# The last tile's second to fourth quarter stores, split by partitions

## The chip, the cores and the metric

The kernel runs on one core of one Trainium2 chip. The metric is the device time of one execution, in microseconds. The time before is 134.82 us, the median of 8 runs that lie between 134.19 and 135.21 us.

A core has five engines that take instructions: TensorE (PE in the profile), VectorE (DVE), ScalarE (ACT), GpSimd (POOL) and SyncE (SP). Transfers between the on-chip memory and DRAM are issued from SP, ACT and POOL, and are carried out by 16 DMA engines that all three share. In the profile, q1 is SP's DMA queue, q10 ACT's, and q0 POOL's; q8 and q14 carry fetches of instructions.

## The reference

Two arrays of 1024 matrices of 64 x 64 are multiplied matrix by matrix:

```python
"a": np.random.randn(1024, 64, 64).astype(np.float32)
"b": np.random.randn(1024, 64, 64).astype(np.float32)
np.matmul(a, b).astype(np.float32)
```

The inputs are 16.8 MB each and so is the output.

## The kernel before

The batch is cut into 16 tiles of 64 matrices. The matrix `b` is loaded a tile at a time (`load_b`, line 96, 1 MB, in turn on SP's and ACT's queue), and `a` two tiles at a time (`load_a`, lines 73 and 77; three quarters of it by POOL with a cast to bf16, one quarter by SP). `regroup` casts and reorders `a`; `transpose` turns it on TensorE and ScalarE copies the result out of PSUM (line 123); `spread` (line 133) writes it on VectorE into a block-diagonal tile; `cast` (lines 144, 149 and 151) makes the bf16 copy of `b`. `multiply` then runs 64 matrix multiplications for a tile into PSUM (line 189), and `evacuate` (line 177) copies the results to the tile's output buffer `o_sb` in on-chip memory, with ScalarE or VectorE.

The order of the work on each engine is the order in which the code is written (`tc.manual_schedule()`). Stores lag one tile behind: after tile t is multiplied, tile t-1 is stored, and tile 15 is stored at the very end.

A tile's output buffer has 128 partitions of 8 blocks (`gh`), each of 1 KB per partition. Tiles 0 to 13 are stored whole, 1 MB each, by POOL. Tile 14 is stored as two halves of 512 KB by SP. The last tile, 15, is multiplied in four quarters of two blocks each, copied out in turn by ScalarE and VectorE, and it is stored as four quarters of 256 KB:

```python
def store_queue(t, lo):
    if t < n_t - 2:
        return nc.gpsimd
    return nc.scalar if t == n_t - 1 and lo % 4 == 0 else nc.sync
```

So quarters 0 and 2 (`lo` of 0 and 4, copied out by ScalarE) are issued by ACT, and quarters 1 and 3 (`lo` of 2 and 6, copied out by VectorE) by SP. The order in which SP takes them is: tile 14's first half, its second half, quarter 1, quarter 3. ACT takes quarter 0 and then quarter 2. All stores are issued on line 166.

The completion of a transfer is counted on a semaphore. Those issued from SP and ACT share eight of these (named DMAHW0 to DMAHW7 in the built program), which are handed out in turn in the order of the program; a transfer that is given one that was used before waits, on its issuing engine, until the earlier transfer of that semaphore has landed. At the end of the program (line 282), SP waits for all of them in a fixed order, and then all engines meet in a closing barrier.

Of the kernel before, what the change touches and what calls it, by code (L numbers as in the profile page):

```python
# [13 lines left out]
def kernel(  # L14
# [27 lines left out]
    o_v = out.rearrange("(t gh x) (mo w) n -> t (x mo) gh (w n)", gh=8, x=8, w=4)  # L42
# [21 lines left out]
# [4 lines that stand above are left out]
# [90 lines left out]
    def multiply(t):  # L158
        at_bd = bd_tiles[t % N_BD][:].rearrange("p j g wl h mo -> p j g (wl h mo)")
        at_bd = at_bd.bitcast(bf16).rearrange("p j g (c u) -> p j g c u", u=2)  # L160
        b_bf = bbf_tiles.pop(t)
        last = t == n_t - 1
        o_sb = o_pool.tile([128, 8, 2, 2, 64], fp32, name="o_sb")

        def put(lo, n):
            store_queue(t, lo).dma_start(  # L166
                out=o_v[t, :, lo : lo + n, :],
                in_=o_sb[:, lo : lo + n].rearrange("p gh j wl n -> p (gh j wl n)"),
            )

        def evacuate(o_ps, gh, n, copies):

            for par in range(2):
                for wl in range(2):
                    src = o_ps[64 * wl : 64 * wl + 64, :, par, :, :]
                    dst = o_sb[64 * par : 64 * par + 64, gh : gh + n, :, wl, :]
                    copies[2 * par + wl](dst, src)  # L177

        for half in range(2):
            if not last:  # L180
                o_ps = o_psum.tile([128, 4, 2, 2, 64], fp32, name="o_ps")
            for g8 in range(8):
                if last and g8 % 4 == 0:
                    o_ps = t_psum.tile([128, 2, 2, 2, 64], fp32, name="at_ps")
                g = 8 * half + g8
                gl = (g8 % 4 if last else g8) // 2
                for j in range(2):
                    for u in range(2):
                        nc.tensor.matmul(  # L189
                            o_ps[:, gl, g % 2, j, :],  # L190
                            at_bd[:, j, g, :, u],
                            b_bf[:, g, 64 * u : 64 * u + 64],
                            start=(u == 0),
                            stop=(u == 1),
                        )
                if last and g8 % 4 == 3:
                    copy = nc.scalar.copy if g8 == 3 else nc.vector.tensor_copy
                    evacuate(o_ps, g // 4 * 2, 2, [copy] * 4)
            if not last:
                copies = [nc.scalar.copy] * 4  # L200
                if half and t % 2:
                    copies[2:] = [nc.vector.tensor_copy] * 2
                evacuate(o_ps, 4 * half, 4, copies)
        if last:
            held[t] = [lambda q=q: put(2 * q, 2) for q in range(4)]
        else:
            whole = t < n_t - 2
            held[t] = [lambda q=q: put(q, 8 if whole else 4) for q in ([0] if whole else [0, 4])]

    with tc.manual_schedule():  # L210
# [18 lines left out]
        for t in range(n_t):  # L229
            s, half = t // 2, t % 2  # L230
            if t + 1 < n_t:
                spread(t + 1)
                cast(t + 1)
            if t + B_AHEAD < n_t:
                load_b(t + B_AHEAD)
            if half == 0 and 0 < s < n_s - 1 - A_AHEAD:
                load_a(s + 1 + A_AHEAD)
            if half == 0 and 0 < s < n_s - 1:
                transpose(s + 1, 1)
            multiply(t)  # L240
            if t == 0:
                regroup(1)
                load_a(A_AHEAD)
                load_a(A_AHEAD + 1)
                transpose(1, 0)
                transpose(1, 1)
            elif t == 1:
                regroup(2)
            elif half == 0 and s + 2 < n_s:
                regroup(s + 2)  # L250
            if half == 1 and s + 2 < n_s:
                transpose(s + 2, 0)
            if t >= HOLD - 1:
                store(t - HOLD + 1)
# [32 lines left out]
```

## Time and profile before

| | |
|---|---|
| time of the profiled execution | 134.82 us |
| its span, first to last instruction | 133.0 us |
| median of 8 runs | 134.82 us (134.19 to 135.21) |
| busy share of the span: PE, DVE, ACT, POOL | 48%, 70%, 66%, 25% |
| mean of DMA traffic over the span | 338 GB/s |
| last tile's last copy | 125.29 to 125.65 us |
| last tile's stores, issue to landing (median) | 7.4 us from SP, 5.6 us from ACT |

How to read it: "busy" counts the time in which an engine works on instructions, while instructions that only issue a transfer or wait are not counted. The DMA row of the page cuts the span into 40 slices and gives the mean busy share of the 16 DMA engines in tenths, 9 standing for 90% or more. The waits name which engine stood still, at which line, and what it was waiting for. The order of time lists instructions by their start, with the time they took; `SPq` and `ACTq` are the issues of transfers on those engines. An answer on DMA for a stretch gives the same kind of 40 digits for that stretch, the rate of each slice, and how many packets were smaller than a given size. Behind these views lie the records of single packets (queue, start, duration, size) and of each step by which a transfer's semaphore went up as its parts landed. The records do not say which of the 16 DMA engines carried a packet.

### The profile page before, as it was taken

To read this page: it belongs to the slowest core of one execution; us is meant where nothing else is said; L and a number is where in the kernel's file an instruction comes from. 1 tells how busy PE (TensorE), PEld (TensorE's weight loads), DVE (VectorE), ACT (ScalarE), POOL (GpSimd) and SP (SyncE) were. 2 spreads that over 40 slices of the span, in tenths; PEclk is the share of its full clock that TensorE was granted. 3 is DMA by queue.
4 is the path that set the end of the run, shared out by engine and by line. 5 is a ranking of instruction groups with operands and counts; after the bars stand their busy time and mean duration, and the time that the engine had idled before them with its cause. 6 is when DMAs were issued, how large, how long until landed. Compare 5 with 4: busy or idle time off the path is not lost.

```text
span 133.0 us, 2837 instructions
## 1 busy us (share of the span) xinstructions
PE 63.2 (48%) x1152; PEld 59.9 (45%) x1152; DVE 93.6 (70%) x120; ACT 87.9 (66%) x161; POOL 32.7 (25%) x43
## 2 busy tenths in 40 slices
PE   0008205960079375279436961866098355761000
PEld 0008105950079374179336961855097354761000
DVE  5621599008999809896899799969999995989000
ACT  3333314999126999959495979696969969089700
POOL 8981000320082070452123003202120402220000
PEclk9999965797557999856985599599959955599555
DMA  3999999999999999999999999999999999999990
GB/s 71 390 329 309 307 296 288 277 305 326 328 326 396 307 318 353 392 384 386 316 278 381 405 390 341 307 321 389 395 393 387 398 392 390 402 405 398 384 343 31
DMA packets 19021, 45.01 MB, mean 338 GB/s; under 512 B 1088, under 2 KB 3136, under 8 KB 19008
## 3 DMA queue, kind: packets, MB, share of 16 engines
q0 software_dynamic: 6832, 20.19, 50.3%
q1 hardware_dynamic: 7120, 14.68, 30.1%
q10 hardware_dynamic: 5056, 9.96, 20.2%
q8 instruction: 9, 0.15, 0.4%
q14 instruction: 4, 0.03, 0.1%
HBM read 33.55 MB, written 16.78 MB: 378 GB/s over the span
## 4 chain that ended last, share of the span: by engine, by line
DMA 54%; DVE 15%; ACT 13%; PE 6%; issue 5%; SPq 1%; ACTq 0%; DVEq 0%
DMA b_sb<-in_b_dram 54%; ACT o_sb L177 9%; DVE at_bd L133 7%; PE o_ps L189 4%; DVE b_bf L144 4%; DVE o_sb L177 3%; PE at_ps L120 2%; ACT at_sb L123 2%; ACT b_bf L144 1%; SPq L90 1%; DVE a_bf L108 1%; ACT b_bf L151 1%; DVE a_bf L111 0%; SPq L96 0%; DVEq L144 0%
## 5 line engine op out<-in xcount | busy, mean ns | idle before, releaser
L177 ACT COPY o_sb<-o_ps 64x512 f32<-64x512 f32 x106 | 61.5, 580 | 10.6 <-PE o_ps L189 9.3
L189 PEld LDWEIGHTS <-at_bd 128*128 128x128 bf16 x1024 | 41.8, 112 | 41.5 <-DVE b_bf L144 26.5
L189 PE MATMUL o_ps<-b_bf,at_bd 128*128 128x64 bf16 x960 | 42.2, 215 | 37.2 <-DVE b_bf L144 24.6
L133 DVE COPY at_bd<-at_sb 32x1024 f32<-32x1024 f32 x64 | 47.4, 741 | 13.5 <-ACT at_sb L123 11.4
L166 POOL DMA_DIRECT2D out_dram<-o_sb x14 | 15.7, 1124 | 58.5 <-ACT at_sb L123 22.7
L120 PE MATMUL at_ps<-identity,a_bf 128*128 128x128 f32 x128 | 20.5, 328 | 18.8 <-DVE a_bf L105 10.6
L120 PEld LDWEIGHTS at_ps<-identity,a_bf 128*128 128x128 f32 x128 | 18.5, 174 | 18.9 <-issue 18.9
L123 ACT COPY at_sb<-at_ps 128x512 f32<-128x512 f32 x32 | 17.5, 589 | 11.3 <-PE at_ps L120 8.5
L144 DVE CAST b_bf<-b_sb 128x2048 bf16<-128x2048 f32 x14 | 17.4, 1245 | 9.6 <-DMA b_sb<-in_b_dram 9.4
L73 POOL DMA_DIRECT2D a_sb<-in_a_dram x21 | 12.9, 628 | 25.3 <-DVE a_bf L108 19.0
L177 DVE COPY o_sb<-o_ps 64x512 f32<-64x512 f32 x14 | 9.6, 689 | 0.3
L108 DVE COPY a_bf<-a_sb 128x3072 bf16<-128x3072 bf16 x7 | 6.7, 953 | 0.0
L144 ACT CAST b_bf<-b_sb 128x2048 bf16<-128x2048 f32 x1 | 1.9, 1898 | 4.7 <-DMA b_sb<-in_b_dram 4.7
L105 ACT CAST a_bf<-o_sb 128x1024 bf16<-128x1024 f32 x2 | 2.1, 1044 | 4.2 <-DMA o_sb<-in_a_dram 4.2
L111 DVE CAST a_bf<-a_raw 128x1024 bf16<-128x1024 f32 x7 | 4.8, 686 | 0.0
L105 DVE CAST a_bf<-o_sb 128x1024 bf16<-128x1024 f32 x2 | 1.5, 772 | 3.7 <-DMA o_sb<-in_a_dram 3.7
L217 DVE MEMSET at_bd<- 128x4096 f32 x1 | 3.5, 3472 | 0.8 <-issue 0.8
L177 DVE COPY o_sb<-at_ps 64x256 f32<-64x256 f32 x8 | 3.4, 422 | 0.5 <-PE at_ps L189 0.4
L151 ACT CAST b_bf<-b_sb 128x512 bf16<-128x512 f32 x2 | 1.1, 616 | 3.4 <-DMA b_sb<-in_b_dram 3.4
L177 ACT COPY o_sb<-at_ps 64x256 f32<-64x256 f32 x8 | 2.9, 366 | 0.1
L214 ACT ACT_TABLE_LOAD x1 | 1.3, 1283 | 2.1 <-issue 2.1
L189 PE MATMUL at_ps<-b_bf,at_bd 128*128 128x64 bf16 x64 | 2.0, 194 | 1.1 <-DVE at_bd L133 1.1
(12 smaller groups left out, 6.1 us busy)
## 6 DMA issues: line engine op xcount, KB each, us to landing
out_dram<-o_sb POOLq DMA_DIRECT2D x14, 1024.0 KB, 21.4
a_sb<-in_a_dram POOLq DMA_DIRECT2D x21, 256.0 KB, 15.8
a_raw<-in_a_dram SPq DMA_DIRECT2D x7, 512.0 KB, 18.5
o_sb<-in_a_dram SPq DMA_DIRECT2D x2, 512.0 KB, 6.9
o_sb<-in_a_dram ACTq DMA_DIRECT2D x2, 512.0 KB, 5.8
out_dram<-o_sb SPq DMA_DIRECT2D x2, 512.0 KB, 7.3
out_dram<-o_sb SPq DMA_DIRECT2D x2, 256.0 KB, 7.4
out_dram<-o_sb ACTq DMA_DIRECT2D x2, 256.0 KB, 5.6
```

Of the source, the lines that this page charges most:

```text
L73: nc.gpsimd.dma_start(out=a_sb[:, h, :, :].rearrange("p v k -> p (v k)"), in_=a_v[s, h])
L105: copy(a_bf[:, :, h, :], a_sb[h].rearrange("p (v k) -> p v k", v=16))
L108: nc.vector.tensor_copy(a_bf[:, :, 0:3, :], cast_sb[:].rearrange("p h v k -> p v h k"))
L111: nc.vector.tensor_copy(a_bf[:, :, 3, :], raw[:])
L120: nc.tensor.transpose(at_ps[:, vo, :], a_cols[:, 4 * vo + 2 * j + wl, :], identity[:])
L123: nc.scalar.copy(at_tiles[s][:, j, :, wl, :, :], at_ps[:].rearrange("p vo (g mp) -> p g mp vo", mp=4),)
L133: nc.vector.tensor_copy(bd[rows, :, :, :, h, :].rearrange("p j g wl mo -> p j (g wl) mo"), at_tiles[t // 2][rows, :, half, :, :, :].rearrange(
L144: (nc.vector.tensor_copy if t else nc.scalar.copy)(b_bf[:], b_sb[:])
L166: store_queue(t, lo).dma_start(out=o_v[t, :, lo : lo + n, :], in_=o_sb[:, lo : lo + n].rearrange("p gh j wl n -> p (gh j wl n)"),)
L177: copies[2 * par + wl](dst, src)
L189: nc.tensor.matmul(o_ps[:, gl, g % 2, j, :], at_bd[:, j, g, :, u], b_bf[:, g, 64 * u : 64 * u + 64], start=(u == 0), stop=(u == 1),)
L217: nc.vector.memset(bd_tiles[0][:], 0.0)
```

## The change

Inside `multiply`, the helper `put`, which issues a store, gets a table of cuts by partition. For the last tile, quarter 1 is stored as partitions 0 to 119 and 120 to 127; quarter 2 as partitions 0 to 125 and 126 to 127; quarter 3 as partitions 0 to 119, 120 to 126, and 127. Quarter 0 and all other tiles are stored as before. The pieces of one quarter are issued one after the other from the same engine, so SP issues five transfers for the last tile in place of two, and ACT three in place of two. The bytes that are written are the same.

```diff
         def put(lo, n):
-            store_queue(t, lo).dma_start(
-                out=o_v[t, :, lo : lo + n, :],
-                in_=o_sb[:, lo : lo + n].rearrange("p gh j wl n -> p (gh j wl n)"),
-            )
+
+            cuts = {2: [0, 120, 128], 4: [0, 126, 128], 6: [0, 120, 127, 128]}.get(
+                lo if last else 0, [0, 128]
+            )
+            for p0, p1 in zip(cuts[:-1], cuts[1:]):
+                store_queue(t, lo).dma_start(
+                    out=o_v[t, p0:p1, lo : lo + n, :],
+                    in_=o_sb[p0:p1, lo : lo + n].rearrange(
+                        "p gh j wl n -> p (gh j wl n)"
+                    ),
+                )
```

In the built program the last stores then stand in this order, with the semaphore that each is counted on and the one that it waits for, beside the copies:

```
SP   tile 14, first half     counted on DMAHW3
SP   tile 14, second half    counted on DMAHW4
SP   quarter 1, 120          counted on DMAHW5
ACT  quarter 0, 128          counted on DMAHW6
SP   quarter 1, 8            counted on DMAHW7, waits for its earlier transfer (a load of b)
ACT  quarter 2, 126          counted on DMAHW0, waits for its earlier transfer (a load of b)
SP   quarter 3, 120          counted on DMAHW1, waits for its earlier transfer (a load of b)
ACT  quarter 2, 2            counted on DMAHW2
SP   quarter 3, 7            counted on DMAHW3, waits for tile 14, first half
SP   quarter 3, 1            counted on DMAHW4, waits for tile 14, second half
```

SP's closing waits stand in the order DMAHW0 to DMAHW7, in both programs. Before, quarter 3 was counted on DMAHW0, quarter 2 on DMAHW7.

## The prediction

> **What bounds the kernel now.** I read the page first, for the totals, then only the tail, because every edited instruction is issued after 123 us of a span of 133.0 us. No instruction ahead of that is moved; the built order of the changed kernel differs from that of before in the last stores of SP and ACT alone. The page's sections 1, 2 and 6 of the kernel before:
>
> ```profile
> span 133.0 us, 2837 instructions
> DMA  3999999999999999999999999999999999999990
> out_dram<-o_sb SPq DMA_DIRECT2D x2, 256.0 KB, 7.4
> out_dram<-o_sb ACTq DMA_DIRECT2D x2, 256.0 KB, 5.6
> ```
>
> The transfers are busy to the last slice but one, and the four quarter stores (256 KB each) take 5.6 to 7.4 us to land. The next view is the order of time from 118 us on:
>
> ```profile
> 120.25 5.44 SPq L166 DMA_DIRECT2D out_dram<-o_sb  x4
> ...
> 124.16 0.40 ACTq L166 DMA_DIRECT2D out_dram<-o_sb  x1
> 124.53 1.12 ACT L177 COPY o_sb<-at_ps 64x256 f32<-64x256 f32 x3
> 125.68 0.38 ACTq L166 DMA_DIRECT2D out_dram<-o_sb  x1
> ```
>
> The last copy and the last issue are over by 126.1. The waits from 117 us on say what follows:
>
> ```profile
> SPq L282 <- DMA out_dram<-o_sb: 5.9, 1, 5.9
> ```
>
> SP, which ends the kernel, stands 5.9 us for stores. The DMA view of 128:130 and then of 130:131 and 131:132 shows how they end:
>
> ```profile
> DMA  9999999999988988977788967687765677644555
> ...
> DMA  2442612111121010101101011010110101011010
> DMA packets 50, 0.04 MB, mean 44 GB/s; under 512 B 7, under 2 KB 50, under 8 KB 50
> ...
> DMA packets 10, 0.01 MB, mean 8 GB/s; under 512 B 2, under 2 KB 10, under 8 KB 10
> ```
>
> Digits are tenths of 16 engines. They thin out after 128.3, and from 130.3 there is one packet of 1 KB at a time, 42.4 ns after the one before in the packet records: one engine works alone. The packets under 512 B are completion marks, and a store of 128 partitions leaves 16. By the landing records 15 marks of the last SP store land from 128.39 to 129.995 and the 16th at 131.686; of the last ACT store the 15th lands at 130.679 and the 16th at 131.386. The late engine already was 1.05 us behind on the last 1 MB store (125.472 against 126.526), after one 16 KB instruction fetch of 1.01 us at 122.10 that some engine carries. After the landing at 131.686 SP runs its remaining waits, about 0.061 us each, and the closing barrier: 1.342 us to 133.028.
>
> **The change, part by part.** The profiled execution took 134.82 us, which is the median of the eight runs too; 133.03 of it is span and 1.79 lies around it.
>
> *Fewer rows on the late engine.* At 16 marks and 256 packets of 1 KB, an engine carries 16 packets (8 partitions by 2) of a quarter store. Per engine the tail holds 32+32 packets of tile 14's two 512 KB stores and 4 times 16, 128 in all. 120 partitions cannot be dealt to 16 engines in equal whole shares; 15 engines by 8 can. 126 is 14 by 9. No row of before shows how such a store is dealt, so I bound it: at best the late engine is left out of all three large pieces and loses 48 x 0.0424 = 2.04 us; at worst it loses none and gains 2+2+2 packets of the small pieces and some of the larger share, at most 9 packets, 0.38 us. I take the best end, since the equal share is what all rows show, and keep the other as a rival. The engines that take over end at the next-latest landing, 130.679, plus at most 9 x 0.0424 = 0.38: 131.06. Were that all, the gain would be 131.69 - 131.06 = 0.63 us.
>
> [...]
>
> *Three more issues on SP, one on ACT.* Issues in the tail took 0.378 to 0.400 us where nothing stood ahead, and 1.215 and 1.275 where two did. The 8-partition piece stands ahead of the fourth quarter on SP (issued at 124.48), which so moves by 0.38 to 1.28 us, to 125.8 at most. The fastest engine lands its second quarter at 126.986, so it still has rows queued: cost nothing, the cover is some 1.2 us. If that cover went, an early engine would idle, and these have 1 to 3 us to spare. ACT's 2-partition issue (about 0.4, to 126.5) has only ACT's closing drain behind it.
>
> *A wait that is new.* SP and ACT stores count completions on eight counters used in turn. The built order of the changed kernel gives the 7-partition piece the counter of tile 14's first 512 KB store and the 1-partition piece that of the second, and each waits until that store has landed. The waits of the 8-, 126- and 2-partition pieces and the fourth quarter's are on transfers that landed by 116.7. Behind the 7-partition wait stands the 1-partition piece, behind that only SP's closing waits. The first store landed at 127.647, the second at 129.825, both last on the late engine. Two packets of the third quarter on the late engine's ACT ring ran ahead of that landing; without them it comes 2 x 0.0424 = 0.085 us sooner, 129.74. Then the wake-up, 0.017 (copy's signal at 120.237, SP's issue at 120.254): 129.76.
>
> From there a new transfer starts from nothing. Issue to first packet: 1.43 us for the first load on ACT's queue with idle engines (issued 0.74, packet at 2.18), 2.01 for ACT's first quarter and 2.72 for SP's first half store, both with engines full. By 129.8 to 131 the engines are nearly idle, so the 1.43 row is nearest; 0.643 of it is the issue, which in the tail is 0.378, and that gives 1.17. I take the middle, 1.30, and keep 1.17 and 2.72. Two packets and a mark are 0.05, mark to landing 0.34 (131.347 to 131.686): 129.76 + 1.30 + 0.05 + 0.34 = 131.45, later than the 131.06 of the other engines, so this piece ends last.
>
> [...]
>
> *A shorter close.* Before, the last counter stood third in SP's list, with seven waits behind it; now it stands seventh, with three behind. 4 x 0.061 = 0.244 us goes: 1.342 becomes 1.098.
>
> Sum: 131.45 + 1.10 = 132.55, against 133.03: 0.48 us less, 134.34 in time; I say 134.4. Gain of the relief 0.63, of the close 0.24, given back by the wait 0.39.
>
> **Rivals.**
> 1. *The new wait eats the relief.* With a first packet at 1.5 to 2.1 us the landing is 131.65 to 132.25, and the change is -0.28 to +0.32 us: 134.55 to 135.15. For it: 2.01 is a store's row. Against: that row had full engines.
> 2. *Slower through the new wait.* With issue to landing of over 2.17 us it is later than before, with over 2.58 by more than 0.3%. The 2.72 row gives 129.76 + 2.72 + 0.39 + 1.10 = 133.97: +0.94 us, 135.8. For it: SP's queue, an empty ring, a store. Against: at 122 every engine moved 4 KB packets. An issue of 1.2 us in place of 0.38 would give 135.1.
> 3. *The split doesn't relieve the late engine.* It stays at 131.69 to 132.07; the last counters then stand earlier in the list (close 1.28), and the end is 132.97 to 133.35: 134.8 to 135.1. For it: the trace doesn't name the late engine. Against: nothing but the equal share.
>
> **How the numbers follow.** About 0.3% (0.40 us) is what a measurement here can tell from none. Forecast 0.42 (134.4); rival 1 0.25; rival 2 0.20; rival 3 0.13, of which 0.11 is within and 0.02 over. So faster 0.42, same 0.25 + 0.11 = 0.36, slower 0.20 + 0.02 = 0.22. Low end: first packet at 1.17 gives 134.2, less 0.3 for the scatter of a median (before spans 134.19 to 135.21): 133.9. High end 135.4, which takes in rivals 1 and 3 and the milder part of 2; its upper half, 0.1, is left out, as is some 0.08 below. The forecast's own range is 133.9 to 134.45.
>
> **What would show it.** Relief: the 120-partition stores leave 15 marks, and no engine works alone at 1 packet per 42 ns until 131.3. Wait: SP stands some 2 us on the second half store at its last store's line, and the last packets are two of 1 KB on SP's queue near 131.1, after a stretch without any. Close: 1.10 us from the last landing to the end. Wrong would be: a first packet over 2 us after the last issue; the late engine still last; or an instruction fetch elsewhere, since the lag of 1 us hangs on it.

## The result, and the profile after

The changed kernel takes 136.18 us (median of 11 runs, 135.37 to 136.64) against 134.82 us: the ratio is 1.0094 with a 95% interval of 1.0078 to 1.011, so it is 1.05 to 1.48 us slower. The forecast was 134.4 with a range up to 135.4; the result lies above it. The profiled execution of the changed kernel took 135.71 us, 0.47 us under its median, so its trace shows 0.89 us of the loss.

The page of the changed kernel, section 1 (span), the DMA row of section 2 and the last tile's larger stores in section 6:

```profile
span 133.9 us, 2842 instructions
...
DMA  3999999999999999999999999999999999999981
...
out_dram<-o_sb SPq DMA_DIRECT2D x2, 240.0 KB, 6.9
out_dram<-o_sb ACTq DMA_DIRECT2D x1, 256.0 KB, 7.0
```

The last line is quarter 0, which the change does not touch. It takes 7.0 us to land; before, the two ACT stores took 5.6 (quarter 0 alone 5.48). The order of time of the changed kernel from 118 us on:

```profile
120.29 10.58 SPq L171 DMA_DIRECT2D out_dram<-o_sb  x7
122.67 1.89 ACT L184 COPY o_sb<-at_ps 64x256 f32<-64x256 f32 x5
124.20 0.41 ACTq L171 DMA_DIRECT2D out_dram<-o_sb  x1
124.57 1.12 ACT L184 COPY o_sb<-at_ps 64x256 f32<-64x256 f32 x3
125.72 2.10 ACTq L171 DMA_DIRECT2D out_dram<-o_sb  x2
```

The copies stand where they stood (to 0.04 us). SP's issues now reach to 130.9 in place of 125.7, ACT's to 127.8 in place of 126.1. What moved in that time is in the DMA answers for 127 to 129 us, the kernel before first:

```profile
DMA  9999999999999999999999999999999889889777
DMA packets 752, 0.72 MB, mean 362 GB/s; under 512 B 45, under 2 KB 752, under 8 KB 752
```

```profile
DMA  9996899989984996994699689977996797986999
DMA packets 555, 0.53 MB, mean 267 GB/s; under 512 B 33, under 2 KB 555, under 8 KB 555
```

The packets of q1 and q10 together took 92% of the 16 engines' time in place of 103.5% (packets of 46 ns that start 42.4 ns apart overlap, so it can exceed 100%), but a quarter less is moved. In the packet records, 203 of the tail's 2048 packets of 1 KB take over 50 ns, the longest 275, against 23 of 2048 and at most 115 ns before; what they take above 46 ns is 10.5 us of engine time in sum (0.65 for each of 16 engines) against 0.5 us. The end of the changed kernel, the answers for 131:132 and 132:133:

```profile
DMA  3542434243322323133242221221111101010110
DMA packets 94, 0.08 MB, mean 84 GB/s; under 512 B 12, under 2 KB 94, under 8 KB 94
...
DMA  1011010110100000000000000000000000000000
DMA packets 8, 0.01 MB, mean 7 GB/s; under 512 B 1, under 2 KB 8, under 8 KB 8
```

From 131.76 on one engine works alone again, until 132.31. Its last 16 packets are on SP's queue, and its mark lands at 132.641: it is the 120-partition piece of quarter 3. The 126-partition piece of quarter 2 landed last at 131.962, 0.679 us or 16 packets of 0.0424 sooner. From 130.862 us on the packets of the engine that ends last can be followed one by one: 18 on ACT's queue, 16 on SP's, each 42.4 ns after the one before, and a completion mark behind each of the two groups. That is a full share of the 126 (9 partitions of 2 KB) and of the 120 (8 partitions). So the engine that ends last is not left out of either piece.

The landing records also show how each piece was dealt. Besides one step that comes soon after the issue, the 120s leave 15 steps, the 126 leaves 14, and the pieces of 8, 7, 2 and 1 partitions leave 8, 7, 2 and 2. In these pieces that is the largest number up to 16 that divides the partitions, and for the 1 partition the number of its blocks. A step is read as one engine's share: the engine that was followed left one mark behind its 18 packets (252 / 14) and one behind its 16 (240 / 15). The later cuts agree by the packets under 512 B on their pages, of which the page of before has 1088: 1152 in sixteen, half64 and ninety_six (seven pieces of 16 marks in place of three), 1128 in sixty (15, 15, 14, 14, 15 and 15), 1101 in q3_spare (7, 7 and 15). Which of the engines they are, no record here names.

### The profile page after: what moved, and what is told of

The parts are those of the page before. It is cut to its first block, busy times and chain, and to the rows that moved or that the text cites. A ratio compares the mean times of both kernels' runs of the same rounds, so it can differ in the third digit from the quotient of the medians.

```text
span 133.9 us, 2842 instructions
## 1 busy us (share of the span) xinstructions
PE 63.0 (47%) x1152; PEld 59.7 (45%) x1152; DVE 93.5 (70%) x120; ACT 87.9 (66%) x161; POOL 32.7 (24%) x43
## 4 chain that ended last, share of the span: by engine, by line
DMA 54%; DVE 17%; ACT 10%; PE 6%; issue 5%; SPq 2%; DVEq 0%; ACTq 0%
DMA b_sb<-in_b_dram 54%; DVE at_bd L133 9%; ACT o_sb L184 7%; DVE o_sb L184 4%; PE at_ps L120 3%; DVE b_bf L144 2%; ACT at_sb L123 2%; PE at_ps L196 2%; ACT b_bf L144 1%; PE o_ps L196 1%; SPq L90 1%; DVE a_bf L108 1%; DVE a_bf L111 0%; SPq L96 0%; DVEq L144 0%
## 5 line engine op out<-in xcount | busy, mean ns | idle before, releaser
L196 PEld LDWEIGHTS <-at_bd 128*128 128x128 bf16 x1024 | 40.4, 110 | 41.5 <-DVE b_bf L144 26.3
L196 PE MATMUL o_ps<-b_bf,at_bd 128*128 128x64 bf16 x960 | 40.7, 212 | 37.1 <-DVE b_bf L144 24.4
L120 PE MATMUL at_ps<-identity,a_bf 128*128 128x128 f32 x128 | 21.7, 342 | 18.9 <-DVE a_bf L105 10.7
L171 POOL DMA_DIRECT2D out_dram<-o_sb x14 | 15.8, 1128 | 59.1 <-ACT at_sb L123 23.2
L120 PEld LDWEIGHTS at_ps<-identity,a_bf 128*128 128x128 f32 x128 | 19.8, 183 | 19.0 <-issue 19.0
```

The source lines that it names most:

```text
L120: nc.tensor.transpose(at_ps[:, vo, :], a_cols[:, 4 * vo + 2 * j + wl, :], identity[:])
L171: store_queue(t, lo).dma_start(out=o_v[t, p0:p1, lo : lo + n, :], in_=o_sb[p0:p1, lo : lo + n].rearrange("p gh j wl n -> p (gh j wl n)"),)
L196: nc.tensor.matmul(o_ps[:, gl, g % 2, j, :], at_bd[:, j, g, :, u], b_bf[:, g, 64 * u : 64 * u + 64], start=(u == 0), stop=(u == 1),)
```

## The experiments

Theory D said that the pieces' packets take longer because of how they are dealt to engines. Theory W said that the issues and waits on SP cost the time. Theory L said that the late engine just carries more rows. The first four runs do one part alone, or all issues and waits without a cut by partitions. In all of them the changes of time are worked out from the ratio and the kernel before of the same session.

**Quarter 1 alone, quarter 2 alone, quarter 3 alone** (`q1_only`, `q2_only`, `q3_only`):

```diff
-cuts = {2: [0, 120, 128], 4: [0, 126, 128], 6: [0, 120, 127, 128]}
+cuts = {2: [0, 120, 128]}          # q1_only
+cuts = {4: [0, 126, 128]}          # q2_only
+cuts = {6: [0, 120, 127, 128]}     # q3_only
```

> Only quarter 1 is cut (120 and 8). No piece waits for a store of tile 14. Theory D (pieces that are dealt to 15, 14, 8, 7 or 2 engines have packets that take longer, and the late engine is not the one left out): between a fourth and a half of the loss, +0.3 to +0.6 us on the kernel before, and some 50 to 100 packets of 1 KB in the tail that take over 50 ns (before: 23, changed kernel: 203). Theory W (SP's extra issues and the new waits of the 7- and 1-partition pieces cost the time): +0.0 to +0.2 us, one issue of up to 1.3 us moved ahead of quarter 3, and no wait. Theory L (the late engine only carries more rows): 0 to 2 more packets, under +0.1 us.

> Only quarter 2 is cut (126 and 2), on ACT. Theory D: +0.3 to +0.6 us, long packets on ACT's queue. Theory W: 0.0 us, as nothing stands behind ACT's last piece. Theory L: the late engine has 18 packets in place of 16 here, +0.1 us.

> Only quarter 3 is cut (120, 7 and 1). The counters fall otherwise than in the changed kernel: the 7- and the 1-partition piece wait for loads that landed long before. Theory D: +0.3 to +0.6 us with long packets on SP's queue. Theory W in its form 'the wait for tile 14's stores': 0.0 us; in its form 'more issues on SP': up to +0.5 us. Theory L: under +0.1 us.

Measured: q1_only 1.0018 [1.0004, 1.0032], +0.24 us, 101 long packets (over 50 ns). q2_only 0.9998 [0.9980, 1.0017], no change, 85 long packets. q3_only 1.0025 [1.0007, 1.0043], +0.34 us, 134 long packets. Long packets come with each part, as theory D said, but quarter 1's cost a little less than its 0.3 to 0.6 us, quarter 2's cost nothing, and the three add up to 0.55 us where all together cost 1.27. So the count of long packets is not the price by itself; most of the gap between 0.55 and 1.27 lies behind the last landing, as the table below shows.

**The same issues, counters and waits, without a cut by partitions** (`blocks`, the code shortened):

```diff
-for p0, p1 in zip(cuts[:-1], cuts[1:]):
-    store_queue(t, lo).dma_start(out=o_v[t, p0:p1, lo : lo + n, :], ...)
+pieces = [(lo, lo + 1, 0, 256), (lo + 1, lo + 2, 0, 256)]              # quarters 1, 2
+pieces = [(6, 7, 0, 256), (7, 8, 0, 128), (7, 8, 128, 256)]            # quarter 3
+rows = o_sb[:].rearrange("p gh j wl n -> p gh (j wl n)")
+for g0, g1, c0, c1 in pieces:
+    store_queue(t, lo).dma_start(out=o_v[t, :, g0:g1, c0:c1], in_=rows[:, g0:g1, c0:c1])
```

> The same number of pieces on the same queues, counters and waits as in the changed kernel, but each of 128 partitions: quarters 1 and 2 are cut into their two blocks of 1 KB per partition, quarter 3 into one block and two halves of a block (512 B). Theory D: every engine carries its 8 partitions as before, no more long packets than before, so the time is within 0.3 us of the kernel before, or up to +0.4 us where the 512 B halves cost. Theory W: as slow as the changed kernel, +1.0 to +1.6 us. Theory L: like before.

Measured: 0.9990 [0.9976, 1.0004], -0.13 us, 9 long packets. Its order of time and its DMA answer for 127 to 129 us:

```profile
120.59 9.53 SPq L174 DMA_DIRECT2D out_dram<-o_sb  x7
124.49 0.41 ACTq L174 DMA_DIRECT2D out_dram<-o_sb  x1
126.01 1.58 ACTq L174 DMA_DIRECT2D out_dram<-o_sb  x2
```

```profile
DMA  9999999999999999999999999999999999879799
DMA packets 784, 0.73 MB, mean 367 GB/s; under 512 B 62, under 2 KB 784, under 8 KB 784
```

SP's issues stretch over 9.5 us here too, and its last piece waits for tile 14's second half (landed at 129.76, piece issued at 129.78, landed at 131.94), yet 367 GB/s are moved and the time is not longer. The last landing comes 0.26 us later than before (131.94 against 131.69), and the stretch from it to the end takes that back: 1.10 us in place of 1.34, as SP has fewer waits left behind that counter. Theory W falls.

**Other cuts by partitions** (`sixteen`, `half64`) **and the large pieces alone** (`big_only`):

```diff
+cuts = {2: [0, 112, 128], 4: [0, 112, 128], 6: [0, 96, 112, 128]}   # sixteen
+cuts = {2: [0, 64, 128], 4: [0, 64, 128], 6: [0, 64, 96, 128]}      # half64
+cuts = {2: [0, 120], 4: [0, 126], 6: [0, 120]}                      # big_only
```

> Quarters 1 and 2 are cut into 112 and 16 partitions, quarter 3 into 96, 16 and 16: as many pieces, in the same places, counters and waits as in the changed kernel, but each count of partitions can be dealt to 16 engines in equal whole shares, so every engine carries as many rows as in the kernel before. Theory D1 (a piece that is cut by partitions has longer packets, however many engines it is dealt to): over 100 packets of 1 KB of more than 50 ns, and +0.7 to +1.6 us. Theory D2 (only the deal to 15 or 14 engines lengthens packets) and theory L (only uneven shares cost): at most 40 such packets and within 0.3 us of the kernel before.

> The same with halves of the partitions: 64 and 64, 64 and 64, 64 and 32 and 32. All on 16 engines. Theory D1: at least as many long packets as with 112 and 16, since each piece covers only half of the partitions at a time, and +0.7 us or more. Theory D2 and theory L: within 0.3 us of the kernel before.

> The small pieces (8, 2, 7 and 1 partitions) are left out: those rows of the last tile's output are not written. The pieces of 120, 126 and 120 partitions stay, and with them four stores in the tail as before, with no new issue or wait. The theory that the large pieces' long packets cost the time: +0.7 to +1.4 us and over 120 long packets. The theory that the small pieces cost it (their issues of up to 1.9 us on SP, their waits): 0.0 to +0.3 us.

Measured: sixteen 1.0107 [1.0071, 1.0143], +1.44 us; half64 0.9995 [0.9978, 1.0011], no change; big_only 1.0079 [1.0052, 1.0105], +1.07 us. All three have long packets: 168, 207 and 184.

big_only shows that the large pieces cause most of the loss, 1.07 us [0.70, 1.42] of 1.27 [1.05, 1.48], without the small ones. sixteen has equal loads on all 16 engines (16 marks for each piece, by its page's 1152) and loses as much: theories L and D2 fall. And half64 breaks D1: it has as many long packets and the same number of pieces and waits, and loses nothing. The DMA answers for 127 to 129 us, sixteen first and then half64:

```profile
DMA packets 676, 0.64 MB, mean 321 GB/s; under 512 B 50, under 2 KB 676, under 8 KB 676
```

```profile
DMA packets 587, 0.55 MB, mean 277 GB/s; under 512 B 46, under 2 KB 587, under 8 KB 587
```

The one that costs nothing moves less in this stretch. A lower rate of all engines together (277 GB/s against 362 before, at an unchanged time) is therefore not what sets the end here. The page's section 6 of the two, sixteen first, has the difference at the uncut quarter 0 (256 KB):

```profile
out_dram<-o_sb ACTq DMA_DIRECT2D x1, 256.0 KB, 6.5
```

```profile
out_dram<-o_sb ACTq DMA_DIRECT2D x1, 256.0 KB, 6.3
```

That is too little to carry the verdict; the last landing does (132.80 against 132.09 us in the two traces).

**The fetch of instructions** (`pe_fewer`, `late_fetch`, `no_fetch`, and the two last with the cuts: `late_fetch_cut`, `no_fetch_cut`). In the kernel before one engine is late after the 16 KB fetch that starts at 122.10 us and takes 1.01: the last 1 MB store has its 15th landing at 125.472 and its 16th at 126.526, 1.05 us later. Theory P said that the cuts cost their time on that engine, theory A that they lengthen all engines' work.

```diff
-for u in range(2):
+for u in range(1 if t == 3 and g < 4 else 2):      # pe_fewer
+for u in range(1 if t == 3 else 2):                # no_fetch, no_fetch_cut
...
+idle_ps = t_psum.tile([128, 4, 128], fp32, name="at_ps")     # late_fetch, late_fetch_cut
+for i in range(18):
+    nc.tensor.transpose(idle_ps[:, i % 4, :], identity[:], identity[:])
```

> The kernel before with 8 matrix multiplications of tile 3 left out (half of the products of its first four groups), so TensorE's program is 16 instructions shorter and the fetch of instructions (16 KB) that takes one DMA engine for 1.0 us at 122 us may fall away or move. If that fetch makes the late engine late: without it the 16th landing of the last 1 MB store is within 0.3 us of the 15th (1.05 us before), and the time falls by 0.6 to 1.0 us. If the fetch stays where it is, this tells nothing. If it goes and the late engine stays, the lag has another cause.

> The kernel before, with 18 transposes of the identity added at the end of TensorE's program, whose result nobody reads. TensorE then ends at about 130 us in place of 120.4, and the 16 KB fetch that has followed its end by 1.7 us in every trace moves from 122 to about 131.5 us, behind the stores. If that fetch makes one engine late, the 16th landing of the last 1 MB store comes within 0.3 us of the 15th (before: 1.05 us), and the last store lands at 130.4 to 130.9 in place of 131.7; the time itself falls by 0.0 to 0.8 us, since TensorE now joins the closing barrier late. If the lag has another cause, the 16th landing stays 1 us behind and the last store lands near 131.7.

> The changed kernel with the same 18 transposes. Theory P (the longer packets of the pieces cost what they cost on the engine that the fetch makes late, the others have room for them): without the late engine the last store lands within 0.4 us of that of the same run without the cuts, near 131, or with the 1-partition piece, which is issued after tile 14's second half has landed (some 1.8 us after 128.2). Theory A (the cuts lengthen the work of all engines alike): the last store still lands 0.7 to 1.3 us after that of the run without the cuts.

> The kernel before with 32 matrix multiplications of tile 3 left out (half of its products), so TensorE's program is 64 instructions shorter. The last 16 KB fetch comes 16 instructions later where 16 are left out and doesn't move where work is added behind it, so it hangs on a place in the program; 64 instructions less should leave that place beyond the program's end. If that fetch makes one engine late: the 16th landing of the last 1 MB store within 0.3 us of the 15th (1.05 us before), the last store at 130.4 to 130.9 us and the time 0.6 to 1.0 us lower. If it does not: the 16th landing stays 1 us behind and the time is that of the kernel before. If the fetch is still there, this tells nothing.

> The changed kernel with the same 32 multiplications left out. Theory P (the longer packets of the pieces cost what they cost on the late engine, the others have room): without a late engine the changed kernel is within 0.4 us of the run without the cuts. Theory A (the cuts lengthen the work of all engines alike): it stays 0.7 to 1.4 us above the run without the cuts, whatever the fetch does.

Measured without the cuts: 1.0001 [0.9984, 1.0017], 1.0001 [0.9990, 1.0011] and 1.0007 [0.9996, 1.0018]. With the cuts: late_fetch_cut 1.0094 [1.0068, 1.0121], no_fetch_cut 1.0088 [1.0065, 1.0110]. The fetch did not go. It came at 122.45, 121.60 and 123.05 us, in late_fetch ahead of the added transposes (124.01 to 127.53) and not behind the end of TensorE's work. The DMA answer for 122:125 of no_fetch still has it, with q8:

```profile
q8 instruction: 1, 0.02, 2.2%
q14 instruction: 1, 0.01, 0.8%
```

The lag stayed: in no_fetch the 16th landing of the last 1 MB store came at 126.58, the 15th at 125.67. As the expectations of pe_fewer and no_fetch say, a fetch that is still there tells nothing, and so nothing is settled between theories P and A: theory P's forecasts were for a kernel without a late engine. With the cuts, the last store landed 1.57 us later in late_fetch_cut than in late_fetch (133.41 against 131.84), above the 0.7 to 1.3 of theory A, and no_fetch_cut took 1.10 us more than no_fetch, inside its 0.7 to 1.4. What these runs add is that the loss of the cut comes again in two more programs.

**Neighbouring partitions per engine, or the number of engines** (`sixty`, `ninety_six`) **and rows off the late engine** (`q3_spare`):

```diff
+cuts = {2: [0, 60, 120], 4: [0, 56, 112], 6: [0, 60, 120]}          # sixty
+cuts = {2: [0, 96, 128], 4: [0, 96, 128], 6: [0, 96, 112, 128]}     # ninety_six
+cuts = {6: [0, 49, 98, 128]}                                        # q3_spare
```

> Partitions 120 to 127 of quarters 1 and 3 and 112 to 127 of quarter 2 are left out (not written). Quarters 1 and 3 go as 60 and 60, quarter 2 as 56 and 56: dealt to 15 and 14 engines as the large pieces of the changed kernel, but with 4 partitions to an engine at a time in place of 8 or 9. Theory R (what costs is the number of neighbouring partitions that one engine takes of a piece: 4 costs nothing as with 64, 7 to 9 costs): within 0.3 us of the kernel before, or below it for the rows left out. Theory E (what costs is that the deal is to 15 or 14 engines): +0.8 to +1.2 us, as with the large pieces alone.

> Quarters 1 and 2 as 96 and 32, quarter 3 as 96, 16 and 16: 16 engines, equal loads, 6 partitions to an engine in the large pieces, with the places, counters and waits of the changed kernel. Theory R: between the 64 (no loss) and the 112 (+1.4 us), so +0.4 to +1.4 us. Theory E: within 0.3 us.

> Quarters 1 and 2 whole as before; quarter 3 as 49, 49 and 30 partitions, which with equal whole shares go to 7, 7 and 15 engines. If the late engine is not one of the first seven, as the marks of the 7- and the 8-partition piece say, it has 2 partitions of quarter 3 in place of 8, and ends some 12 packets (0.5 us) sooner; the first seven have 16 packets more (0.7 us) and end at 131.4 at most. Theory P (the last engine alone sets the end): -0.2 to -0.5 us in time, less what 7 partitions to an engine cost (up to +0.3). If the late engine is one of the first seven: +0.5 to +0.9 us. Theory A (all engines' work sets the end): +0.3 us.

Measured: sixty 0.9993 [0.9978, 1.0007], no change, 136 long packets; ninety_six 1.0080 [1.0051, 1.0108], +1.08 us, 193; q3_spare 1.0039 [1.0025, 1.0054], +0.53 us, 119. sixty deals to 15 and 14 engines like the changed kernel (1128 marks on its page) and loses nothing; ninety_six deals to 16 (1152) and loses 1.08. Theory E falls, theory R fits. The rows left out do not excuse sixty: big_only leaves rows out as well and loses 1.07. A rival to theory R stands untested: in half64 and sixty all pieces have at most 64 partitions, in the kernels that lose a microsecond the large ones have 96 to 126. So it may be the size of the piece, or which partitions it spans, and not the number that one engine takes. Only q3_spare parts the two (pieces of 49, 7 to an engine), and there seven engines also carry more rows.

q3_spare was slower. Its +0.53 lies in what was expected if the late engine were one of the first seven, but 7 neighbouring partitions per engine may cost something too, and q3_only lost 0.34 with 8; theory A had +0.3. The marks had pointed to an engine outside the first seven: in the changed kernel the last mark of the 7-partition piece lands at 132.242, before that of quarter 3's 120 at 132.641, though it was issued after it. But that pieces on fewer engines go to the same first ones, as "one of the first seven" supposes, was an assumption: no record names the engines. Which engine is late stays open.

**The side on which packets are held up** (`stride_whole`, `stride_cut`):

```diff
-out=o_v[t, :, lo : lo + n, :]
...
+flat = out[64 * t : 64 * t + 64].rearrange("b m n -> (b m n)")
+dst = flat.rearrange("(e p q c) -> p q e c", e=2, p=128, q=4)[:, lo // 2]     # both
...
+cuts = {2: [0, 112, 128], 4: [0, 112, 128], 6: [0, 96, 112, 128]}            # stride_cut
```

> The kernel before, with the last tile's four quarters written to other places of its 1 MB in DRAM: neighbouring partitions 4 KB apart in place of 1 KB, still in pieces of 1 KB (the last tile's output is in another order). It is the base for the next run. Both theories: within 0.3 us of the kernel before, unless the new distance costs by itself.

> The same order in DRAM, with the quarters cut into 112 and 16, 112 and 16, and 96, 16 and 16 partitions. Theory S (the longer packets arise on the side of the on-chip memory, where engines that take 6 to 9 neighbouring partitions each meet at the same partitions' outlets): as with the same cut before, +0.7 to +1.6 us on the run without the cut, and over 100 packets of 1 KB that take over 50 ns. Theory M (they arise in DRAM, where engines write at distances of 6 to 9 KB): with distances four times as large the cost is another one, within 0.4 us of the run without the cut, and at most 60 such packets.

Measured: stride_whole 1.0006 [0.9992, 1.0020] with 17 long packets, stride_cut 1.0086 [1.0061, 1.0111] with 239; the difference of the two is +1.08 us. Changing the distance in DRAM by four did not lower the cost, and theory M's forecast, a cost of at most 0.4 us and at most 60 long packets, failed. It is not a proof of theory S: the distances of the tried order are one choice of many, and no record shows on which side a packet is held up, or an outlet at which engines meet.

The DMA answers for 127 to 129 us, stride_whole first and then stride_cut, show the rate fall again with the cut:

```profile
DMA packets 769, 0.74 MB, mean 372 GB/s; under 512 B 43, under 2 KB 769, under 8 KB 769
```

```profile
DMA packets 585, 0.56 MB, mean 279 GB/s; under 512 B 40, under 2 KB 585, under 8 KB 585
```

And those for 130 to 132 us show what is left over by then, sixty first and then ninety_six (digits are tenths of 16 engines): sixty is done at 131.4, ninety_six goes on to 132 and beyond.

```profile
DMA  6756542332112111111111111110000000000000
DMA packets 142, 0.12 MB, mean 61 GB/s; under 512 B 23, under 2 KB 142, under 8 KB 142
```

```profile
DMA  6876956663344364342211111111000010000001
DMA packets 242, 0.19 MB, mean 96 GB/s; under 512 B 54, under 2 KB 242, under 8 KB 242
```

The runs side by side. "Row run" is the number of partitions that one engine takes of the large pieces, by equal whole shares (that they are neighbours is assumed; no record names them); the packets are those of 1 KB in the tail, counted from the packet records of the profiled execution; the rate is that of 127 to 129 us; "quarter 0" is issue to landing of the uncut quarter 0; "close" is the time from the last landing to the end of the span.

| kernel | row run | change, us | over 50 ns | over 140 ns | GB/s | quarter 0, us | close, us |
|---|---|---|---|---|---|---|---|
| before | whole store | 0 | 23 | 0 | 362 | 5.5 | 1.34 |
| blocks | whole store | -0.13 [-0.32, 0.05] | 9 | 0 | 367 | 5.5 | 1.10 |
| half64 | 4 | -0.07 [-0.30, 0.15] | 207 | 8 | 277 | 6.3 | 1.09 |
| sixty | 4 | -0.09 [-0.30, 0.09] | 136 | 2 | 290 | 5.8 | 1.16 |
| q2_only | 9 | -0.03 [-0.27, 0.23] | 85 | 4 | 341 | 5.4 | 1.21 |
| q1_only | 8 | 0.24 [0.05, 0.43] | 101 | 17 | 320 | 6.5 | 1.28 |
| q3_only | 8 | 0.34 [0.09, 0.58] | 134 | 6 | 335 | 6.0 | 0.92 |
| q3_spare | 7 and 2 | 0.53 [0.34, 0.73] | 119 | 10 | 314 | 5.5 | 1.22 |
| ninety_six | 6 | 1.08 [0.69, 1.46] | 193 | 25 | 286 | 7.0 | 1.09 |
| sixteen | 7 and 6 | 1.44 [0.96, 1.93] | 168 | 36 | 321 | 6.5 | 1.10 |
| big_only | 8 and 9 | 1.07 [0.70, 1.42] | 184 | 41 | 280 | 7.2 | 0.91 |
| changed | 8 and 9 | 1.27 [1.05, 1.48] | 203 | 30 | 267 | 7.0 | 1.29 |

Where all three quarters are cut, the row run divides the kernels that lose (6 to 9) from those that don't (4). The number of packets over 50 ns and the rate do not divide them. The packets over 140 ns do: at most 8 where nothing is lost, 25 to 41 where a full microsecond is. Among the kernels with one cut they do not (q3_only has 6 and q1_only 17, and q3_only loses no less). That was seen afterwards, in one execution of each, and no run was made to test it.

The close differs from kernel to kernel, since it depends on how many of SP's closing waits stand behind the counter that holds the end up: 1.342 us with seven behind it in the kernel before, 1.095 with three in blocks. So the change of time hides a part of what a cut does to the landing. With the shortening of the close added, as the one profiled execution of each has it, quarters 1, 2 and 3 alone cost 0.30, 0.10 and 0.76 us, 1.16 in sum, against 1.32 for all three together; the large pieces alone cost 1.50, no less than all pieces together. half64 then has 0.18, sixty 0.09 and blocks 0.11, still far from the 1.3 to 1.7 of ninety_six and sixteen.

## Why the prediction was wrong, point by point

**Fewer rows on the late engine.** This step failed first. The prediction took the best end, in which the late engine is left out of the three large pieces and loses 2.04 us. That 15 or 14 engines take the large pieces was right; that the late one is among those left out had no row for it. The engine that ends last carries quarter 2's and quarter 3's share one after the other, 18 and 16 packets, with landings at 131.962 and 132.641. If it is also the one that landed tile 14's second half last (129.784), it had quarter 1's share as well: that landed last at 130.446, again 16 packets (0.66 us) on. Rival 3 said so and was given 0.13, but its sum ended at 135.1, and the kernel took 136.18: a second term was wrong.

**The price of a packet.** The prediction counted every packet at 0.0424 us, in pieces as in whole stores, and so priced rival 3 at no more than 9 packets. No row of before had a piece of fewer than 128 partitions, and the deal was bounded but the pace was not. This is the term that was missing: the large pieces alone cost 1.07 us in time. Where the late engine lost it can be read in part. From the last landing of tile 14's second half to the last landing of all took 2.86 us (129.784 to 132.641), before 1.86 (129.825 to 131.686). If one engine has all the last landings, it still had its shares of quarters 1, 0, 2 and 3 to carry at 129.784 (they land last at 130.446, 131.209, 131.962 and 132.641): 66 packets, 2.80 us at the old pace. Before, 1.86 us has room for 44. So from there on it kept the old pace and was some 22 packets or 0.93 us behind, of the 0.955 by which the last landing moved; 2 of the 22 are its larger share of quarter 2. The rest it must have lost earlier, and most of the time that the tail's packets took above 46 ns, 8.0 of 10.5 us, falls before 129.45 us, where the mark of that landing was sent. Only its last 34 packets are followed one by one; the rest of this reading is an argument, not an experiment. The runs show the cut as the cause, not the path along the engine.

**More issues.** The bound was 1.28 us for an issue with others ahead; the 8-partition piece took 1.58, quarter 3's 120 took 1.91 and was issued at 126.22, beyond the 125.8 foreseen. ACT's last two took 0.91 and 1.16. That more issues cost no time was right: blocks has as many, on the same queues, and is not slower.

**The new wait.** The wait is there: in blocks the last piece was issued at 129.78, 0.02 us after tile 14's second half landed. The sizes were nearly right: in the changed kernel tile 14's second half landed at 129.784 (forecast 129.74), the 1-partition piece took 1.788 us from issue to landing (forecast 1.30 + 0.05 + 0.34 = 1.69). It was issued only at 130.121, as the 7-partition issue ahead of it ran until 130.07, a delay of 0.32 that the prediction had not counted. It landed at 131.91 (forecast 131.45), 0.73 us ahead of the last landing: it did not end last, so rivals 1 and 2 did not decide the time. But 131.91 lies in rival 1's range (131.65 to 132.25): with the close of 1.10 the end would have been 133.01 against 133.03. Even with the late engine relieved, the forecast gain would have gone.

**The shorter close.** With quarter 3's 120 last, the last counter is DMAHW1, and the close took 133.927 - 132.641 = 1.286 us. Rival 3 had 1.28 for that case. The forecast's own case, the last landing on DMAHW4, came in blocks: 1.095 us against the 1.098 forecast. So this step was right, and its condition did not come about.

## What to carry to other kernels

A store that is cut by partitions is dealt to the DMA engines anew (here 120 partitions left 15 marks where 128 left 16), and its packets need not keep the pace of the whole store's (203 of 2048 took over 50 ns in place of 23); measure one piece before counting its rows at the old pace. If a large store has to be cut, cut it along the free dimension with all 128 partitions in each piece, or into halves that give an engine 4 partitions: here both were free (-0.13 us [-0.32, 0.05] and -0.07 [-0.30, 0.15]), and large pieces with 6 to 9 cost 0.8% to 1.1% where all three quarters were cut so. And where one engine ends late, find out whether the cut leaves out that engine before the gain is counted.

## What the runs showed of the hardware that was not expected

Packets of 1 KB, which take 46 ns in the median of the tail before and 115 at most, took up to 275 ns in the changed kernel, 30 of its 2048 over 140 ns. With neighbouring partitions 4 KB apart in DRAM in place of 1 KB the cut had such packets too: 239 over 50 ns in stride_cut, 17 in stride_whole.

The scatter was larger in the kernels that lose: the runs of sixteen spread over 1.73 us (135.69 to 137.42) and those of the changed kernel over 1.27, those of blocks over 0.53. Those of half64, which loses nothing, spread over 1.05, through a single run.

Open is what makes a packet long, and on which side for certain; whether the partitions per engine or the size of the piece decides; which engine is late; and whether the fetch of instructions makes it so.
